# A one-layer hybrid encoder step: the raw weight loads of the projections go from SyncE's queue to POOL's

## The chip, the core and the metric

The kernel runs on one core of a Trainium2 chip. The metric is the time of one execution on the device in microseconds (us). Before the change three runs took 3268.99, 3278.84 and 3281.25 us; their median is 3278.84 us.

## The reference, cut to what matters

One step of a one-layer model on a prompt of 2048 tokens and a sample of 32 tokens, width 1024. Every matrix product with a weight is computed in float32 quality.

```python
z = rmsnorm(x, norm_mix_g) @ w_in                      # 1024 x 2560
q, k, v, zr = split(z, (512, 640, 768))
a_out = window_attention(q, k, v, ...)                 # 8 heads, windows of 64-token chunks
r_out, shift, S = rwkv7_mixer(zr, ...)                 # 8 heads, a recurrence over all tokens
x = x + concat(a_out, r_out) @ w_out                   # 1024 x 1024
x = x + memory_cross_attention(rmsnorm(x), mk, mv)     # w_cq 1024 x 512, w_co 512 x 1024
x = x + square(relu(rmsnorm(x) @ w_up)) @ w_down       # 1024 x 4096, 4096 x 1024
y = rmsnorm(x, norm_final_g)
```

The memory's keys and values are `rmsnorm(mem) @ w_mk` and `rmsnorm(mem) @ w_mv`. The recurrence `rwkv7_mixer` is serial over the tokens.

## The kernel before, in words

The 2080 tokens are kept transposed, width on the partitions. All projections but the MLP's work on four token groups of 512 or 544 tokens (`GROUPS`), each cut into two blocks of 256 or 272 columns. `dense` (line 299) runs one projection: for every weight unit it calls `load_w` (line 252) and then, for both blocks, `mm3` (line 230). A unit is 128 x 1024 numbers. Float32 quality comes from splitting a number into two parts of a shorter type: `mm3` does three matmuls per slice (high x high, high x low, low x high; lines 234 to 236), so a unit of 8 slices and 2 blocks is 48 matmuls into the tile `ps_z`.

`load_w` brings the weights in. For each half of a unit (512 columns) it takes a buffer `w_raw`, of which there are two (`RB` = 2), loads 128 x 512 float32 numbers from HBM by a DMA (line 257), and calls `split` (line 172): ACT copies the tile into the high part `w_h` (line 66), and POOL subtracts it from the raw tile and writes the low part `w_l` (line 69). When POOL is done, the raw buffer is free and its next load may start. The first two units of the kernel's first projection have their subtraction on DVE instead (`fast`). In the MLP `load_w` is called directly, with two raw buffers of its own (`fu`).

`zphase` (line 321) is the projection w_in; `ophase`, `cqphase` and `cophase` are w_out, w_cq and w_co; `memphase` does w_mk and w_mv. `PLAN` (line 35) lists in which sequence these are written down between the recurrence steps (R, `rwkv_tile`, 17 tiles of up to 128 tokens), the attention tiles (A) and the cross-attention jobs (X). Results go to HBM scratch (`zrw`, `zqkv`, `mscr`, `x2scr`, `qscr`, `cscr`, `x3scr`) and are loaded again by the next stage. An RWKV tile has a serial row of small transfers: it loads `zl`, `zin` and `zv`, stores `ab` to `lscr`, loads `lt` from it, stores `xt` to `xscr` and loads `td` from it (lines 533 to 678). On POOL it computes products for the tiles `z` and `bk` (lines 602 to 610) and the state `sn` (line 757), from `tp`, which DVE makes.

All DMAs are issued by SyncE (SP, `Q`). Each engine takes its instructions strictly in order, and so does each issuing queue: an instruction that waits holds all behind it on its engine. In which order the instructions of an engine stand is not the order of the code: a scheduler sets it before the run, by priorities (`setp`) and by its own estimate of when each operand is there. A change of the issuing engine therefore moves rows on all engines. The MLP follows the rest: six blocks of 352 or 320 tokens, `mup` and `mdn`.

Of the kernel before, what the change touches and what calls it, by code (L numbers as in the profile page):

```python
# [38 lines left out]
PSOL, PSER, RB, SNB = "s", "s", 2, 3  # L39
XB, WB, XS = 5, 2, 4  # L40
# [10 lines left out]
def hymba_step_kernel(  # L51
# [9 lines left out]
    V, G, S, T, Q = nc.vector, nc.gpsimd, nc.scalar, nc.tensor, nc.sync  # L61
# [19 lines left out]
    def pmm(name="pmm"):  # L81
        return psmm.tile([P, 512], F32, tag="pmm", name=name, bufs=PSB["pmm"])
# [89 lines left out]
    def split(xt, h, l, eng=None):  # L172
        act(h, xt)
        tt(l, xt, h.bitcast(F32), SUB, eng)
# [55 lines left out]
    def mm3(ps, wh, wl, xh, xl, nk):  # L230
        old = setp("m")
        for k in range(nk):
            a, b, c, d = wh(k), wl(k), xh(k), xl(k)
            T.matmul(ps, lhsT=a, rhs=c, start=(k == 0), stop=False)  # L234
            T.matmul(ps, lhsT=a, rhs=d, start=False, stop=False)  # L235
            T.matmul(ps, lhsT=b, rhs=c, start=False, stop=(k == nk - 1))  # L236
        setp(old)
# [10 lines left out]
    zp = stage1.enter_context(tc.tile_pool(name="zp", bufs=1))  # L248
    rctx = ExitStack()
    rp = rctx.enter_context(tc.tile_pool(name="rp", bufs=1))  # L250

    def load_w(pool, src, n=1024, bufs=3, tag="w", eng=None, rb=RB, raw=None):
        wh = pool.tile([P, n], F32R, tag=tag + "h", name="w_h", bufs=bufs)
        wl = pool.tile([P, n], F32R, tag=tag + "l", name="w_l", bufs=bufs)
        for i in range(0, n, 512):
            w = (raw or pool).tile([P, 512], F32, tag="wraw", name="w_raw", bufs=rb)
            Q.dma_start(w, src[:, i:i + 512])
            split(w, wh[:, i:i + 512], wl[:, i:i + 512], ENG[E7] if eng is G and i else eng)
        return wh, wl

# [38 lines left out]
    def dense(wsrc, units, xs, blks, evac, nk=KC, per=1, rs=None, fast=False):  # L299
        cols = nk * P  # L300
        if rs is None:
            rs = [None] * len(blks)
        for u in units:
            wh, wl = load_w(zp, wsrc[u], bufs=WB, eng=V if fast and u < units[0] + 2 else G)
            for j in range(per):
                ft = u * per + j
                for bi, (b0, nb) in enumerate(blks):
                    if callable(xs[bi]):
                        xs[bi] = xs[bi]()
                    xh, xl, r = xs[bi]  # L310
                    ps = pmm("ps_z")
                    mm3(ps[:, 0:nb], lambda k: wh[:, j * cols + k * P:j * cols + (k + 1) * P],
                        lambda k: wl[:, j * cols + k * P:j * cols + (k + 1) * P],
                        lambda k: xh[k // XS][:, k % XS, 0:nb], lambda k: xl[k // XS][:, k % XS, 0:nb], nk)
                    if rs[bi] is None and r is not None:
                        rs[bi] = r()
                    evac(ft, bi, b0, nb, ps, rs[bi])
# [3 lines left out]
    def zphase(g, units):  # L321
# [12 lines left out]
        def evac(ft, bi, b0, nb, ps, r):  # L334
# [26 lines left out]
            Q.dma_start(zqkv[g][:, ft, b0:b0 + nb] if ft < 6 else zrw[g][:, ft - 6, b0:b0 + nb], zo[:, 0:nb])  # L361

        dense(win, units, xs, blks, evac, rs=rs, fast=(g == 0 and 0 not in units))
        if 0 in units:
            zouts(g)
# [16 lines left out]
    def memphase():  # L382
        lab("mem")
        xs = [prep(memT.rearrange("(k p) t -> p k t", p=P), NMEM, "mem")]

        def evk(h, bi, b0, nb, ps, r):
            zo = zp.tile([P, NH], F32, tag="zo", name="zok", bufs=3)
            tt(zo[:, 0:nb], ps[:, 0:nb], r, MUL)
            Q.dma_start(kxs[:, h], zo[:, 0:nb])
            Q.dma_start(pmkT[:, h], zo[:, 0:nb])  # L390

        def evv(h, bi, b0, nb, ps, r):
            zo = zp.tile([P, NH], F32, tag="zo", name="zov", bufs=3)
            tt(zo[:, 0:nb], ps[:, 0:nb], r, MUL)
            pt = pmm("pvx")
            for m in range(2):
                T.transpose(pt[:, m * P:(m + 1) * P], zo[:, m * P:(m + 1) * P], ident)
            zv_ = zp.tile([P, NH], F32, tag="zo", name="zovt", bufs=3)
            act(zv_[:, 0:nb], pt[:, 0:nb])
            zv3 = zv_[:, 0:nb].rearrange("p (a b) -> p a b", a=2)  # L400
            Q.dma_start(vxs[:, :, h * P:(h + 1) * P], zv3)
            Q.dma_start(pmv[:, :, h * P:(h + 1) * P], zv3)

        dense(wmk, range(4), xs, [(0, NMEM)], evk)
        dense(wmv, range(4), xs, [(0, NMEM)], evv)
# [635 lines left out]
    for s_ in range(start[5] + 16):  # L1041
        up = []
        for i in range(2):
            u = (2 * s_ + i) % 3
            up.append(load_w(fw if u == 2 else fu, wup[2 * (s_ % 16) + i], bufs=1, tag=f"wu{u}", raw=fu))
        dn = [load_w(fw, wdn[2 * (s_ % 16) + i], bufs=3, tag="wd", raw=fu, eng=V)
              for i in range(2)]
        act_b = sorted((b for b in range(6) if start[b] <= s_ < start[b] + 16), key=lambda b: start[b])
        for b in act_b:
            if 0 < b < 3 and s_ == start[b]:  # L1050
                mprep(b)
            lab(f"M{b}.mm")
            us = mup(b, up)
            if s_ == start[b]:
                mres(b)
            if pend is not None:
                flush(pend)
            pend = (b, us, dn, s_ == start[b] + 15)
# [113 lines left out]
```

## Time and profile before

| what | value |
|---|---|
| median of 3 runs | 3278.84 us |
| the profiled execution | 3264.26 us, its span 3262.5 us |
| mean granted clock of TensorE (share of full speed) | 0.964 |
| PE busy | 3031.4 us (93%) |
| DVE busy | 1894.3 us (58%) |
| ACT busy | 1243.9 us (38%) |
| POOL busy | 1014.4 us (31%) |
| DMA, mean | 101 GB/s |

A profile tells for each engine when it worked and, where it stood idle, which other instruction ended the wait. PE is TensorE's matmul, DVE is VectorE, ACT ScalarE, POOL GpSimd, SP SyncE; SPq is SP's issuing queue. "A <- B: 10.0, 4, 3.1" in the view of waits means that A waited 10.0 us in all for B, 4 times, the longest 3.1 us. "out<-in" are the tiles that an instruction writes and reads. The chain of waits is followed back from the last instruction, at each step to what released it; its pieces add up to the span.

### The profile page before, as it was taken

What the parts mean: (1) busy time and instruction counts of PE and PEld (TensorE: products, weight loads), DVE (VectorE), ACT (ScalarE), POOL (GpSimd) and SP (SyncE); (2) the same over time, 40 slices, a digit from 0 to 9 for tenths busy, and PEclk for the clock granted to TensorE, in tenths of its full rate; (3) what the DMA queues carried; (4) which work ended last, traced back from release to release, by engine and by line L of the source; (5) the groups of instructions that cost most, each with busy time, mean ns of one, the idle gap of its engine ahead of it and who ended that gap; (6) DMA issues with size and microseconds to landing.
All of it is one profiled execution on the core that took longest, in us unless ns stands there. A gap on an engine that the chain in (4) does not pass through costs nothing.

```text
span 3262.5 us, 64715 instructions
## 1 busy us (share of the span) xinstructions
PE 3031.4 (93%) x25605; PEld 2837.5 (87%) x25605; DVE 1894.3 (58%) x4482; ACT 1243.9 (38%) x2824; POOL 1014.4 (31%) x1017
## 2 busy tenths in 40 slices
PE   8989888888988998998988999999999999999998
PEld 7877767777766987778877999999999999999998
DVE  4577788877776577764334544444445644444446
ACT  5355465444464454444453321222224322222223
POOL 3443354324254344425554411111113511011111
PEclk9999999999988999899989999999999999999999
DMA  5444353334443454346765211111113211111112
GB/s 170 133 114 109 104 147 110 104 87 123 120 137 101 131 158 127 111 124 195 247 217 171 67 50 42 46 46 52 39 46 115 66 43 52 40 52 52 46 46 91
DMA packets 336752, 328.95 MB, mean 101 GB/s; under 512 B 82320, under 2 KB 256064, under 8 KB 336448
## 3 DMA queue, kind: packets, MB, share of 16 engines
q1 hardware_dynamic: 336448, 324.81, 33.0%
q8 instruction: 201, 3.29, 0.4%
q14 instruction: 103, 0.84, 0.1%
HBM read 252.59 MB, written 72.39 MB: 100 GB/s over the span
## 4 chain that ended last, share of the span: by engine, by line
PE 62%; DVE 15%; DMA 11%; ACT 6%; issue 3%; POOL 2%; SPq 1%; DVEq 0%; POOLq 0%; ACTq 0%
PE ps_up L236 7%; PE ps_dn L1002 7%; PE ps_up L235 7%; PE ps_dn L1003 7%; PE ps_dn L1004 7%; PE ps_up L234 7%; PE ps_z L234 4%; PE ps_z L236 4%; PE ps_z L235 4%; DVE z L69 2%; DMA lt<-lscr 2%; DVE prd L69 1%; DMA lscr<-ab 1%; DMA xb<-x2scr 1%; ACT xh L66 1%
## 5 line engine op out<-in xcount | busy, mean ns | idle before, releaser
L234 PE MATMUL ps_z<-xh,w_h 128*128 128x256 f32 (+1 forms) x2368 | 716.7, 303 | 91.8 <-DVE zo L69 41.5
L235 PE MATMUL ps_z<-xl,w_h 128*128 128x256 f32 (+1 forms) x2368 | 705.9, 298 | 2.0 <-DVE xl L69 1.4
L236 PE MATMUL ps_z<-xh,w_l 128*128 128x256 f32 (+1 forms) x2368 | 704.0, 297 | 0.0
L66 ACT ACTIVATE w_h<-w_raw 128x512 fp32r<-128x512 f32 x576 | 344.7, 626 | 780.6 <-PE ps_up L235 258.5
L69 DVE TENSOR_TENSOR x<-ps_dn,x 128x352 f32<-128x352 f32 (+1 forms) x768 | 389.8, 516 | 367.4 <-PE ps_dn L1004 363.9
L69 POOL TENSOR_TENSOR w_l<-w_raw,w_h 128x512 fp32r<-128x512 f32 x300 | 393.1, 1325 | 608.8 <-ACT w_h L66 585.2
L234 PEld LDWEIGHTS ps_z<-xh,w_h 128*128 128x128 f32 x2368 | 470.4, 199 | 118.9 <-DVE zo L69 40.6
L69 POOL TENSOR_TENSOR rl<-rl 128x352 f32<-128x352 f32 (+1 forms) x192 | 162.1, 845 | 1137.3 <-ACT uh L66 1137.2
L1002 PE MATMUL ps_dn<-uh,w_h 128*128 128x352 f32 (+1 forms) x1536 | 492.9, 321 | 4.4 <-DVE x L69 3.3
L236 PE MATMUL ps_up<-fh,w_l 128*128 128x352 f32 (+1 forms) x1536 | 495.4, 323 | 1.2 <-DVE w_l L69 1.2
L1003 PE MATMUL ps_dn<-ul,w_h 128*128 128x352 f32 (+1 forms) x1536 | 491.0, 320 | 4.9 <-DVE ul L69 4.9
L234 PE MATMUL ps_up<-fh,w_h 128*128 128x352 f32 (+1 forms) x1536 | 493.2, 321 | 0.4 <-DVE zo L69 0.4
L235 PE MATMUL ps_up<-fl,w_h 128*128 128x352 f32 (+1 forms) x1536 | 491.1, 320 | 0.1
L1004 PE MATMUL ps_dn<-uh,w_l 128*128 128x352 f32 (+1 forms) x1536 | 490.7, 320 | 0.0
L235 PEld LDWEIGHTS ps_z<-xl,w_h 128*128 128x128 f32 x2368 | 470.4, 199 | 15.2 <-issue 7.4
L236 PEld LDWEIGHTS ps_z<-xh,w_l 128*128 128x128 f32 x2368 | 469.6, 198 | 15.5 <-issue 10.8
L69 DVE TENSOR_TENSOR w_l<-w_raw,w_h 128x512 fp32r<-128x512 f32 x276 | 198.0, 737 | 218.4 <-ACT w_h L66 217.9
L1003 PEld LDWEIGHTS ps_dn<-ul,w_h 128*128 128x128 f32 x1536 | 289.8, 189 | 5.5 <-DVE ul L69 5.2
L1002 PEld LDWEIGHTS ps_dn<-uh,w_h 128*128 128x128 f32 x1536 | 288.6, 188 | 6.8 <-DVE x L69 3.2
L236 PEld LDWEIGHTS ps_up<-fh,w_l 128*128 128x128 f32 x1536 | 288.4, 188 | 1.7 <-DVE w_l L69 1.5
L1004 PEld LDWEIGHTS ps_dn<-uh,w_l 128*128 128x128 f32 x1536 | 289.2, 188 | 0.2
L234 PEld LDWEIGHTS ps_up<-fh,w_h 128*128 128x128 f32 x1536 | 288.3, 188 | 1.2 <-DVE zo L69 0.6
(245 smaller groups left out, 4489.6 us busy)
## 6 DMA issues: line engine op xcount, KB each, us to landing
w_raw<-in_win SPq DMA_DIRECT2D x160, 256.0 KB, 2.9
w_raw<-in_wup SPq DMA_DIRECT2D x136, 256.0 KB, 2.7
w_raw<-in_wdn SPq DMA_DIRECT2D x136, 256.0 KB, 2.7
w_raw<-in_wout SPq DMA_DIRECT2D x64, 256.0 KB, 3.3
zrw<-zo SPq DMA_DIRECT2D x84, 128.0 KB, 1.9
lt<-lscr SPq DMA_DIRECT2D x34, 244.0 KB, 3.8
zin<-zrw SPq DMA_DIRECT2D x16, 512.0 KB, 3.9
w_raw<-in_wcq SPq DMA_DIRECT2D x32, 256.0 KB, 3.4
```

Of the source, the lines that this page charges most:

```text
L66: S.activation(out, in_, func, **kw)
L69: (eng or V).tensor_tensor(out, a, b, op=op)
L234: T.matmul(ps, lhsT=a, rhs=c, start=(k == 0), stop=False)
L235: T.matmul(ps, lhsT=a, rhs=d, start=False, stop=False)
L236: T.matmul(ps, lhsT=b, rhs=c, start=False, stop=(k == nk - 1))
L1002: T.matmul(ps[:, 0:n], lhsT=wh[:, ms], rhs=us[i][0], start=(i == 0), stop=False)
L1003: T.matmul(ps[:, 0:n], lhsT=wh[:, ms], rhs=us[i][1], start=False, stop=False)
L1004: T.matmul(ps[:, 0:n], lhsT=wl[:, ms], rhs=us[i][0], start=False, stop=(i == 1))
```

## The change

`load_w` gets a parameter `q`, the engine that issues the load of the raw tile. `dense` passes POOL (`G`) for it, and SP (`Q`) only for the first two units of the kernel's first projection. The calls in the MLP don't pass it and stay on SP.

```diff
-    def load_w(pool, src, n=1024, bufs=3, tag="w", eng=None, rb=RB, raw=None):
+    def load_w(pool, src, n=1024, bufs=3, tag="w", eng=None, rb=RB, raw=None, q=None):
         wh = pool.tile([P, n], F32R, tag=tag + "h", name="w_h", bufs=bufs)
         wl = pool.tile([P, n], F32R, tag=tag + "l", name="w_l", bufs=bufs)
         for i in range(0, n, 512):
             w = (raw or pool).tile([P, 512], F32, tag="wraw", name="w_raw", bufs=rb)
-            Q.dma_start(w, src[:, i:i + 512])
+            (q or Q).dma_start(w, src[:, i:i + 512])
             split(w, wh[:, i:i + 512], wl[:, i:i + 512], ENG[E7] if eng is G and i else eng)
...
         for u in units:
-            wh, wl = load_w(zp, wsrc[u], bufs=WB, eng=V if fast and u < units[0] + 2 else G)
+            wh, wl = load_w(zp, wsrc[u], bufs=WB, eng=V if fast and u < units[0] + 2 else G,
+                            q=Q if fast and u < units[0] + 2 else G)
```

SP's queue in the middle of the second group's w_in, before: the raw loads stand between the stores of results (`zo`) and the RWKV transfers.

```order
L655 DMA lscr_160_2407<-ab 64x8x64 x2
L660 DMA lt<-lscr_160_2407 64x976 x2
L257 DMA w_raw<-in_win 128x512
L361 DMA zrw_91<-zo 128x256
L257 DMA w_raw<-in_win 128x512
L797 DMA zq<-zqkv_86 128x4x128
L535 DMA zv<-zrw_90 128x4x32
L801 DMA kc__4098<-zqkv_86 128x128
```

The same RWKV tile on SP's queue after the change (lines after 304 have a number higher by one).

```order
L656 DMA lscr_160_2407<-ab 64x8x64 x2
L661 DMA lt<-lscr_160_2407 64x976 x2
L362 DMA zrw_91<-zo 128x256 x2
L536 DMA zv<-zrw_90 128x4x32
L534 DMA zl<-zrw_90 128x2x128
L362 DMA zrw_91<-zo 128x256
L675 DMA xscr_143<-xt 64x8x16 x2
```

No raw load is left between them, and the stores and loads stand closer together.

POOL in the same phase, before: subtractions of weights (`w_l`), the state `sn`, and RWKV's products.

```order
L69 TENSOR_TENSOR bk<-km,cs 64x8x64 x2
L69 TENSOR_TENSOR w_l<-w_raw,w_h 128x512 x2
L69 TENSOR_TENSOR sn<-tp,pcl 128x256
L69 TENSOR_TENSOR w_l<-w_raw,w_h 128x512 x2
L69 TENSOR_TENSOR sn<-tp,pcl 128x256
L69 TENSOR_TENSOR w_l<-w_raw,w_h 128x512 x4
L69 TENSOR_TENSOR z_4275<-zin,pp 64x4x64
L69 TENSOR_TENSOR z_4276<-zin,pp 64x4x64
L69 TENSOR_TENSOR bk<-kka,cs 64x8x64 x2
```

POOL at the same place after the change.

```order
L257 DMA w_raw<-in_win 128x512 x2
L69 TENSOR_TENSOR sn<-tp,pcl 128x256
L69 TENSOR_TENSOR w_l<-w_raw,w_h 128x512 x2
L257 DMA w_raw<-in_win 128x512 x2
L69 TENSOR_TENSOR w_l<-w_raw,w_h 128x512 x2
L257 DMA w_raw<-in_win 128x512
L69 TENSOR_TENSOR z_4275<-zin,pp 64x4x64
L69 TENSOR_TENSOR z_4276<-zin,pp 64x4x64
L257 DMA w_raw<-in_win 128x512
```

Issues of raw loads now stand on POOL behind the subtraction that frees their buffer, some of them directly in front of `sn` and `z` or behind them.

## Rows read from the trace of the kernel before

**Rows 1.** Busy time by stretch: us, then busy (instructions) by engine, clock, DMA
```profile
core 0: us, PE busy (x) PEld busy (x) DVE busy (x) ACT busy (x) POOL busy (x), PEclk, DMA share, GB/s
0.00:1790.00 1790.00, 1572.02 (x16419) 1384.61 (x16420) 1175.77 (x3155) 864.66 (x2060) 745.86 (x713) 0.94 0.47 138
1790.00:3262.00 1472.00, 1459.43 (x9188) 1452.86 (x9186) 718.48 (x1328) 379.26 (x765) 268.49 (x305) 1.00 0.17 55
```
**Rows 2.** Chain of waits, 0 to 1790 us: shares of the stretch by line
```profile
by line: PE ps_z L234 7.7%; PE ps_z L236 7.3%; PE ps_z L235 7.2%; issue 5.0%; DVE z L69 3.5%; DMA lt<-lscr 3.0%; DVE prd L69 2.2%; DMA lscr<-ab 2.1%; DMA xb<-x2scr 2.1%; ACT xh L66 2.0%; PE pA L225 1.8%; DVE xt L69 1.8%; DVE yb L72 1.5%; DM
```
**Rows 3.** DMA issues: queue, count, size of one, median us from issue to landing
```profile
w_raw<-in_win SPq DMA_DIRECT2D x160, 256.0 KB, 2.9
...
w_raw<-in_wout SPq DMA_DIRECT2D x64, 256.0 KB, 3.3
...
w_raw<-in_wco SPq DMA_DIRECT2D x32, 256.0 KB, 3.4
```
**Rows 4.** Tile w_raw, 0 to 1790 us: min/median/max ns, first to last start
```profile
L66 ACT ACTIVATE w_h<-w_raw x314: 611/624/659, 10.8 to 1789.9; 128x512 fp32r<-128x512 f32 x157
L69 POOL TENSOR_TENSOR w_l<-w_raw,w_h x300: 1257/1288/1809, 26.9 to 1760.8; 128x512 fp32r<-128x512 f32 x150
L257 SPq DMA_DIRECT2D w_raw<-in_win x160: 327/372/1699, 4.8 to 1161.6; - x160
```
**Rows 5.** Waits of SP's queue, 0 to 1790 us: total us, times, longest
```profile
SPq L257 <- POOL w_l L69: 228.0, 141, 7.8
...
SPq L655 <- ACT ab L66: 37.8, 12, 12.1
```
**Rows 6.** Waits of the engines, 0 to 1790 us
```profile
POOL sn L69 <- DVE tp L69: 111.5, 24, 15.3
...
ACT w_h L66 <- DMA w_raw<-in_win: 29.4, 23, 3.5
...
ACT w_h L66 <- DMA w_raw<-in_wout: 20.7, 12, 5.1
...
ACT w_h L66 <- DMA w_raw<-in_wco: 16.4, 11, 3.4
...
ACT w_h L66 <- DMA w_raw<-in_wmv: 9.0, 4, 4.5
...
ACT w_h L66 <- DMA w_raw<-in_wcq: 7.8, 5, 3.3
...
PE ps_z L234 <- ACT w_h L66: 11.9, 2, 11.4
```
**Rows 7.** Chain of waits, 104 to 136 us: start us, us, what
```profile
120.64 1.28 POOL w_l L69
121.94 0.33 SPq L257
...
122.38 2.52 DMA zl<-zrw
```
**Rows 8.** Chain of waits: the first and last moved load, and a blocked one
```profile
104.88 3.43 DMA w_raw<-in_win
...
1549.96 1.30 POOL w_l L69
...
1551.28 0.83 SPq L257
...
1552.16 0.42 SPq L463
...
1641.11 3.88 DMA w_raw<-in_wco
```
**Rows 9.** Groups of DVE instructions, 0 to 1790 us: count, busy us, mean ns
```profile
L853 DVE TENSOR_SCALAR sc<-sc,sm 128x256 f32<-128x256 f32 x120 | 59.5, 549 | 0.7
```
**Rows 10.** The page's costliest groups: busy us, mean ns, idle before
```profile
L234 PE MATMUL ps_z<-xh,w_h 128*128 128x256 f32 (+1 forms) x2368 | 716.7, 303 | 91.8 <-DVE zo L69 41.5
```

## The prediction

> **What bounds the kernel now.** I began with the busy times by stretch [rows 1]. They split the span at about 1790 us. In the second stretch, the MLP, PE is busy for 1459 of 1472 us, and its weight loads keep SP's queue: I take that stretch as unchanged. In the first, 1790 us with all projections, attention and RWKV, PE is busy for 1572 us, at a mean granted clock of 0.94, and idle for 218 us. No engine is full: DVE 1176 us, ACT 865, POOL 746 (42%). This is where the change acts.
>
> The chain of waits over the first stretch comes next [rows 2]. It is spread thin: the three dense matmul lines hold 22%, the rest is RWKV's arithmetic on DVE, PE's small matmuls, and transfers such as the load of the triangular factors (lt, 3.0%). No single wait rules the stretch, so only what lies on this thread counts.
>
> Then the loads of raw weights. A 256 KB load lands a median 2.9 to 3.4 us after its issue [rows 3]. SP spends a median 0.37 us on an issue; the ACT split after it takes 0.62 us, POOL's subtraction 1.29 us [rows 4]. Each half unit goes load, ACT, POOL, and its buffer (two exist) is then free for the next load. SP stands at line 257 until POOL's subtraction frees the buffer: 228.0 us in 141 waits, 1.62 us each, up to 7.8 us [rows 5]. That is the queue blocking which the change takes away. On the other side, ACT already finds a load not landed in 23 + 4 + 12 + 5 + 11 = 55 cases, 83.3 us, while PE itself shows only 11.9 us of waiting for w_h in two cases [rows 6].
>
> **The change, part by part.** It moves 300 issues (156 of w_in, 64 of w_out, 32 each of w_cq and w_co, 8 each of w_mk and w_mv) to POOL. Four first loads and all 272 MLP loads stay.
>
> *SP's queue is freed.* It loses 300 x 0.37 = 111 us of issuing and the 228.0 us of waiting. What of it is on the path? The chain shows two places where another load stands behind a raw load: POOL's subtraction of 1.28 us, then SP's issue of 0.33 us, then the zl load of an RWKV tile [rows 7], and once the same with 1.30 and 0.83 us in front of a cross-attention load [rows 8]. These are 1.6 and 2.1 us: a gain of 4 us. Nothing is the lower bound. The upper one is a mean wait of 1.62 us ahead of one transfer in each of the 17 RWKV tiles, 27 us. I stay with 4, because SP's own rows speak for it: where SP waits for the stores of lscr it has arrived early and waits for ACT (37.8 us) [rows 5], so these stores are not queued behind a raw load.
>
> *A load costs POOL something.* No row shows a DMA issue on POOL. The lower bound is SP's 0.37 us; the upper one is POOL's nearest row, the 1.29 us of the subtraction on the same tile [rows 4]. I take the upper, since it is the same engine and the same tile, and since the issue can't run beside the next subtraction. So each moved load lands 1.29 - 0.37 = 0.92 us later after its buffer falls free. On the chain of the first stretch 15 moved loads stand, the first at 104.88 us and the last at 1641.11 us [rows 8]: 15 x 0.92 = 14 us. The bounds are 0 and the 55 cases in which ACT is already waiting, 55 x 0.92 = 51 us. What hides the other 245 is that they land before ACT comes to them; the cover is gone where the slack was under a microsecond.
>
> The Trainium skill ("DMA: Bandwidth & Descriptors", section "Anatomy of one DMA — SWDGE (gpsimd) path") gives a fit for a DMA issued from this engine, 2.0 us plus the bytes over 436 GB/s, which for 262,144 bytes is an estimate of 2.6 us and so below the 2.9 to 3.4 us that the rows show on SP's queue; by it this term would be 0 rather than 14, and no run before the change can show which.
>
> *POOL gets fuller and is in order.* 300 x 1.29 = 387 us more make 1133 of 1790 us, 63%. The order shows issues put directly in front of RWKV's z products and of the sn step; the same holds for bk. A POOL row then meets an issue in front of it with a chance of 387/1790 = 0.22, and waits half of it, 0.65 us: 0.14 us. With 17 tiles and four such places each (two of z, two of bk), that is 10 us if all are on the path, 0 if none; I take 8, as the chain runs through the products for most tiles. The reverse also holds: a load is queued behind rows that wait. POOL waits for RWKV's tp in front of sn for 111.5 us, 24 times, 15.3 us at worst [rows 6]; the order has four issues directly behind an sn row. I leave this to the rivals.
>
> *The order moves.* The scheduler puts all engines' rows anew, PE's too. That has no price in a row; I allow a tenth of PE's 218 idle us, 22 us, to either side, in the range alone.
>
> The sum is -4 + 14 + 8 = +18 us. The profiled execution took 3264.26 us, 14.6 us under the median of the three runs, 3278.84 us; the change is added to the median: 3297 us.
>
> **Rivals.**
>
> *No change.* The issue on POOL costs little more than SP's, or the later landing is within the slack of the loads; then -4 + 0 + 8 = +4 us, 3283 us. For it: PE waits for a weight split in two cases only, and a dense unit of 48 matmuls of 0.30 us [rows 10] takes 14.5 us, against 2.9 to 3.4 + 0.62 + 1.29, at most 5.3 us, of load, split and subtraction. Against it: the 15 loads on the chain. The fit of the skill's DMA page, above, leads here.
>
> *Faster.* The blocking on SP is worth its upper bound: every RWKV tile gets one transfer 1.62 us earlier, -27 us, and POOL's issues fall into its 1044 us of idle time, 0 us: 3252 us. It decides if SP's wait at line 257 stands in front of one of a tile's serial transfers (zl, lscr, lt, xscr, td) in nearly all tiles. For it: 141 waits in 1790 us, one per 13 us. Against it: the chain shows it once for an RWKV tile.
>
> *Clearly slower: POOL as the blocked queue.* The wait that SP loses comes back on POOL, where it holds compute and loads together. If a third of the 111.5 us that POOL stands in front of sn is passed to loads and to the dense units behind them, 37 us, with the +18 that is +55 us, 3334 us. It decides when loads stand behind sn without a spare buffer; the order has four such places, at most 4 x 15.3 = 61 us.
>
> The Trainium skill ("SBUF — State Buffer", section "SBUF: two separate sides") states besides that a copy or tensor_scalar of DVE within SBUF locks POOL out of the port with which it writes a DMA's descriptors. As a mechanism of this kernel: the largest such DVE row takes 0.55 us, 120 times [rows 9]; 15 chain loads each delayed by a whole one would be 8 us, so 3305 us. I keep it within the slower case.
>
> **How the numbers follow.** Small loss of about 18 us: 0.45. No change: 0.28. Faster: 0.19. Clearly slower: 0.08. A measurement of this kernel can tell about 0.5%, 16 us, from no change, and the likeliest case lies close to that border; 0.08 of its 0.45 I count as ending within it. So faster is 0.19, same 0.28 + 0.08 = 0.36, slower 0.37 + 0.08 = 0.45. The range goes from the faster rival, 3252, to the slower one's 3334, with a few microseconds more at the top, 3338, for the port; the tenth of the idle time on either side of 3297 (3275 to 3319) is inside. The likeliest case's own range is 3283 to 3319.
>
> **What would show it.** In the profile after: the issues of raw loads appear on POOL with a duration (I say 1.29 us, bounds 0.37 and 1.29), and POOL's busy time or its waits grow by about 387 us in the first stretch. SP's wait at line 257 for POOL, 228.0 us, is gone there. ACT's wait for raw loads rises from 83.3 us to about 130. The second stretch stays at 1472 us within a few. The first grows from 1790 to about 1808 us with PE's busy time about the same. I am wrong if POOL's rows show no cost for an issue, if ACT's wait for loads falls, or if the RWKV chain's transfers start visibly earlier.

## The result and the profile after

The changed kernel takes 3293.91 us (median of 9 runs, 3286.76 to 3303.38) and the kernel before 3272.99 us (9 runs, 3267.73 to 3281.25). The ratio is 1.0059, with a 95% interval of 1.0048 to 1.0071: some 19 us slower. I had forecast 3297 us. One execution of pool_issue_three_buffers, a kernel further down, took 4883.40 us at a mean granted clock of 0.628 and is in no ratio.

Busy time by stretch, cut where the MLP's first matmul starts: the kernel before, then the one after (rows as in [rows 1]; the cut was 20 us later there).

```profile
core 0: us, PE busy (x) PEld busy (x) DVE busy (x) ACT busy (x) POOL busy (x), PEclk, DMA share, GB/s
0.00:1770.00 1770.00, 1558.23 (x16352) 1371.99 (x16352) 1156.00 (x3123) 860.44 (x2050) 735.69 (x707) 0.94 0.47 139
1770.00:3262.00 1492.00, 1473.21 (x9254) 1465.48 (x9253) 738.25 (x1360) 383.48 (x774) 278.66 (x311) 1.00 0.17 55
```
```profile
0.00:1797.00 1797.00, 1576.89 (x16352) 1388.87 (x16352) 1181.74 (x3122) 862.37 (x2050) 886.57 (x1007) 0.93 0.46 137
1797.00:3289.00 1492.00, 1473.21 (x9254) 1465.24 (x9253) 738.23 (x1360) 384.03 (x774) 278.20 (x311) 1.00 0.17 55
```

The second stretch is 1492 us in both, to a hundredth in PE's busy time. The whole loss, 27 us in this pair of profiled executions, lies in the first stretch, as forecast. The pair overstates it a little: the profiled execution before is 8.7 us under its kernel's median, the one after 2.4 us. In the first stretch PE executes the same 16352 matmuls, but is busy for 18.7 us more at a mean granted clock of 0.93 for 0.94 (a mixture of its 2.4 and 1.2 GHz levels; the lower one was granted for 256.0 us after and 221.9 us before), and idle for 8.3 us more (220.1 for 211.8). POOL's busy time grows by 150.9 us, DVE's by 25.7 us. That DVE's grows at all was in no step of mine.

The issues and landings of the moved loads come next, from the list of DMA issues (last column: median us from issue to landing) and the tile view of w_raw over the first stretch (min/median/max ns).

```profile
w_raw<-in_win POOLq DMA_DIRECT2D x156, 256.0 KB, 3.3
...
w_raw<-in_wout POOLq DMA_DIRECT2D x64, 256.0 KB, 3.4
...
w_raw<-in_wco POOLq DMA_DIRECT2D x32, 256.0 KB, 4.1
```
```profile
L69 POOL TENSOR_TENSOR w_l<-w_raw,w_h x300: 1255/1284/1742, 26.9 to 1788.4; 128x512 fp32r<-128x512 f32 x150
L257 POOL DMA_DIRECT2D w_raw<-in_win x156: 536/553/796, 19.6 to 1187.2; - x156
```

An issue holds POOL for 0.55 us, where I had said 1.29 [rows 4], and SP's took 0.37. The loads of these three weights land 0.1 to 0.7 us later than in [rows 3] (3.3 for 2.9, 3.4 for 3.3, 4.1 for 3.4 us); those of w_cq and w_mk land as before, at 3.4 and 3.0 us.

Then the waits, ACT's and SP's, over the first stretch (us in total, times, longest).

```profile
ACT w_h L66 <- DMA w_raw<-in_win: 67.5, 37, 9.6
...
ACT w_h L66 <- DMA w_raw<-in_wco: 30.0, 10, 5.9
...
ACT w_h L66 <- DMA w_raw<-in_wout: 17.1, 11, 4.4
...
ACT w_h L66 <- DMA w_raw<-in_wcq: 14.0, 6, 4.9
```
```profile
SPq L656 <- ACT ab L66: 75.2, 21, 14.6
```
```profile
PE ps_z L234 <- ACT w_h L66: 18.8, 4, 11.3
...
PE ps_z L236 <- POOL w_l L69: 5.0, 7, 1.4
```

With 1.5 us for w_mv, ACT stands 130.1 us for raw loads, in 65 cases, where it was 83.3 in 55 [rows 6]. SP's 228.0 us at line 257 [rows 5] are gone, and no gain shows: where SP stands for the data of lscr (line 656) it now does so for 75.2 us instead of 37.8 [rows 5] (49.3 in new_order_sp_issue below, which has the same order). I read this as SP arriving earlier and waiting for ACT. PE's own waits for the two halves of a weight come to 18.8 + 5.0 us; they were 11.9.

### The profile page after: what moved, and what is told of

It reads as the page before. It is cut to its first block, busy times and chain, and to the rows that moved or that the text cites. A ratio compares the mean times of both kernels' runs of the same rounds, so it can differ in the third digit from the quotient of the medians.

```text
span 3289.7 us, 64554 instructions
## 1 busy us (share of the span) xinstructions
PE 3050.1 (93%) x25605; PEld 2854.1 (87%) x25605; DVE 1920.0 (58%) x4482; ACT 1246.4 (38%) x2824; POOL 1164.8 (35%) x1317
## 4 chain that ended last, share of the span: by engine, by line
PE 59%; DVE 17%; DMA 12%; ACT 4%; issue 3%; POOL 3%; SPq 1%; DVEq 0%; ACTq 0%; POOLq 0%
PE ps_up L236 7%; PE ps_up L235 7%; PE ps_dn L1003 7%; PE ps_up L234 7%; PE ps_dn L1005 7%; PE ps_dn L1004 7%; PE ps_z L234 3%; PE ps_z L236 3%; PE ps_z L235 3%; DVE z L69 2%; DMA lt<-lscr 2%; DMA w_raw<-in_win 1%; DVE xt L69 1%; DMA lscr<-ab 1%; DVE prd L69 1%
## 5 line engine op out<-in xcount | busy, mean ns | idle before, releaser
L234 PE MATMUL ps_z<-xh,w_h 128*128 128x256 f32 (+1 forms) x2368 | 720.8, 305 | 116.0 <-DVE zo L69 43.3
L235 PEld LDWEIGHTS ps_z<-xl,w_h 128*128 128x128 f32 x2368 | 475.6, 201 | 19.7 <-issue 11.9
## 6 DMA issues: line engine op xcount, KB each, us to landing
w_raw<-in_win POOLq DMA_DIRECT2D x156, 256.0 KB, 3.3
w_raw<-in_wup SPq DMA_DIRECT2D x136, 256.0 KB, 2.8
w_raw<-in_wdn SPq DMA_DIRECT2D x136, 256.0 KB, 2.6
w_raw<-in_wout POOLq DMA_DIRECT2D x64, 256.0 KB, 3.4
w_raw<-in_wcq POOLq DMA_DIRECT2D x32, 256.0 KB, 3.4
```

## The experiments

The scheduler orders all engines anew when a load changes its queue, so the two kernels differ in more than the change says. To part the two, I fixed the order: a helper ties each instruction to the one ahead of it in a table of instruction numbers, engine by engine, with a dependency that orders but waits for no semaphore.

```diff
+def _pin(tc):
...
+    for engine, steps in json.loads(zlib.decompress(base64.b85decode(ORDER))).items():
...
+            if last is not None:
+                tc.add_manual_dep(i, last.name, dep, reason="pin")
+            last = i
```

"Old order" is that of the kernel before, "new order" that of the changed one. The helper stands ahead of the rest in the file, so that line numbers are higher in these kernels (line 257 is 273 to 279).

All twelve runs, with the ratio to the kernel before on the same chip. "First stretch" is the start of the first ps_up matmul; "ACT waits" is the sum of the rows "ACT w_h <- DMA w_raw" up to there, MLP loads left out; the busy times are the page's, of the whole span.

| kernel | us | ratio, 95% interval | first stretch | ACT waits, us (times) | DVE, POOL busy |
|---|---|---|---|---|---|
| before | 3272.99 | 1 | 1769.8 | 83.3 (55) | 1894.3, 1014.4 |
| after | 3293.91 | 1.0059, 1.0048 to 1.0071 | 1796.8 | 130.1 (65) | 1920.0, 1164.8 |
| old_order_pool_issue | 3312.7 | 1.0127, 1.011 to 1.0144 | 1820.5 | 157.9 (85) | 1915.2, 1167.3 |
| new_order_sp_issue | 3273.55 | 1.0007, 0.9996 to 1.0019 | 1773.9 | 59.0 (38) | 1900.1, 1007.2 |
| old_order_pool_early | 3322.54 | 1.0147, 1.0121 to 1.0173 | 1826.2 | 85.0 (54) | 1944.7, 1176.2 |
| old_order_sp_issue_pool_fill | 3287.74 | 1.0041, 1.0024 to 1.0058 | 1785.4 | 91.4 (57) | 1907.9, 1148.7 |
| new_order_pool_early | 3289.46 | 1.0051, 1.0033 to 1.007 | 1786.5 | 79.5 (47) | 1940.6, 1171.8 |
| old_order_sp_issue_tied | 3315.99 | 1.0133, 1.0112 to 1.0154 | 1817.3 | 174.3 (96) | 1895.6, 1009.2 |
| old_order_sp_issue_tied_fill | 3338.77 | 1.0206, 1.0183 to 1.0229 | 1842.1 | 183.5 (99) | 1904.4, 1145.3 |
| old_order_act_issue | 3288.99 | 1.0049, 1.0029 to 1.0069 | 1789.4 | 68.7 (43) | 1900.0, 1015.8 |
| pool_issue_three_buffers | 3287.9 | 1.0046, 1.0029 to 1.0062 | 1782.9 | 18.5 (20) | 1906.8, 1162.9 |
| sp_issue_three_buffers | 3250.35 | 0.9929, 0.9908 to 0.995 | 1747.3 | 11.7 (7) | 1878.4, 1004.6 |
| three_buffers_pool_order_sp_issue | 3271.71 | 0.9989, 0.9978 to 1.0 | 1765.2 | 6.0 (5) | 1895.4, 1010.5 |
| three_buffers_sp_order_pool_issue | 3281.13 | 1.0013, 1.0 to 1.0026 | 1782.8 | 43.3 (33) | 1886.8, 1160.0 |

### The issue or the order?

**old_order_pool_issue** is the change alone, in the order of the kernel before.

```diff
-            Q.dma_start(w, src[:, i:i + 512])
+            (q or Q).dma_start(w, src[:, i:i + 512])
...
+    _pin(tc)
```

> The order of every engine's rows is pinned to that of the kernel before; only the 300 raw loads are issued by POOL, each at the place in POOL's order at which the scheduler had put it in the whole program before. Theory A (the issue on POOL itself costs: later landings and a POOL row in front of others): 1.004 to 1.007 of the kernel before, +14 to +22 us, and ACT's wait for raw loads near the 129 us of the changed kernel. Theory B (the loss is the scheduler's new order): 0.998 to 1.002 of before. Theory C (SP freed is a gain that the new order hides): under 0.998.

Measured: 1.0127, 40 us slower, above every range that I had given: theory A's direction, at nearly twice its upper bound. **new_order_sp_issue** is the opposite: the changed kernel's order, with the loads on SP (the kernel before with only `_pin` and the table).

> The order of every engine's rows is pinned to that of the changed kernel; the 300 raw loads are issued by SP, each at the place at which the changed kernel's whole program has it. Theory A (the issue on POOL itself costs): 0.998 to 1.002 of the kernel before. Theory B (the new order costs): 1.004 to 1.008 of before. Theory C (the new order costs more than the change shows, and POOL's issue gives some of it back): over 1.008.

Measured: 1.0007, no difference from the kernel before that could be measured, and within theory A's range.

So the issue on POOL is the cause, and the new order by itself costs nothing. In the old order the issue costs 1.27%, in the new one 0.52% (1.0059 - 1.0007). The new order thus gives back 0.0127 - 0.0059 = 0.68%, some 22 us, of the 41 us that the issue costs. By what it gives them back was not shown; a first guess, below, gets no support.

### Which part of the issue?

**old_order_pool_early** moves each load on POOL to directly behind the subtraction that frees its buffer. In the old order 142 of 298 such loads stand behind the other half's subtraction too (two subtractions, then two loads), and in the new order 106; here none does. Only the table changes; POOL's rows where it does:

```diff
 w_l<-w_raw,w_h 128x512
+w_raw<-in_win 128x512
 w_l<-w_raw,w_h 128x512
-w_raw<-in_win 128x512
 w_raw<-in_win 128x512
```

**new_order_pool_early** is the same in the new order.

> The 300 loads are issued by POOL, all other rows of every engine stand in the order of the kernel before, as in old_order_pool_issue (3312.7 us, 40 over the kernel before); but each load stands on POOL directly behind the subtraction that frees its buffer, where there it mostly stood behind both subtractions of the weight (two subtractions, then two loads). Theory Q (queue place): the cost is that the first load of a pair waits on POOL behind the second subtraction (1.33 us and its wait for ACT), so the time falls by 20 us or more, to 3293 or below, with ACT's waits for raw loads near those of the kernel before (below 100 us in the first stretch; 150 with the old places). Theory O (occupancy): POOL's 0.55 us for each issue in front of the other half's subtraction and of other rows is what costs; the place hardly matters, 3305 to 3325 us. Theory L (the later landing alone, 0.3 us each): 3305 to 3315, ACT's waits as with the old places.

> The changed kernel with its own order on every engine, but each load on POOL directly behind the subtraction that frees its buffer. Theory Q: what the scheduler's order had not yet given back comes back, 3275 to 3285 us. Theories O and L: as the changed kernel, 3290 to 3297.

Measured: 1.0147 and 1.0051, in theory O's range (3305 to 3325) and half a microsecond under it (3290 to 3297). ACT's waits for loads fall as theory Q said, from 157.9 to 85.0 us and from 130.1 to 79.5, and the time does not follow: +0.2% in the old order and -0.08% in the new one, both less than the intervals are wide. So "the load comes too late, and that is all" falls, and the guess that the new order is better because fewer loads stand behind a second subtraction gets no support. By my reading, what the early load wins for ACT it takes from POOL, whose second subtraction now stands behind the issue, and from DVE: its busy time grows by another 29.5 us (1915.2 to 1944.7) and 20.6 us (1920.0 to 1940.6). Where that comes from, the last section shows.

The chains of waits of the first stretch fit this. These are new_order_sp_issue and then the changed kernel, which has the same order:

```profile
by line: PE ps_z L250 8.1%; PE ps_z L252 7.9%; PE ps_z L251 7.9%; issue 5.0%; DVE z L85 3.8%; DMA lt<-lscr 3.1%; DMA xb<-x2scr 2.6%; PE pA L241 2.2%; DVE prd L85 2.2%; DVE xt L85 1.9%; DMA lscr<-ab 1.6%; DVE sc L869 1.5%; ACT xh L82 1.5%; D
```
```profile
by line: PE ps_z L234 5.9%; PE ps_z L236 5.8%; PE ps_z L235 5.7%; issue 5.3%; DVE z L69 3.2%; DMA lt<-lscr 3.0%; DMA w_raw<-in_win 2.6%; DVE xt L69 2.5%; DMA lscr<-ab 2.4%; DVE prd L69 2.4%; PE pA L225 2.3%; DVE sc L854 2.3%; POOL w_l L69 2
```

Added up piece by piece, raw loads hold 36.2 us of the first chain (9 loads) and 80.7 us of the second (21), POOL's subtractions 19.1 and 38.8 us, and the issues themselves 5.6 us. In old_order_pool_early the loads are down to 47.5 us (12), but the subtractions stand at 41.5 us and the issues at 9.7. This is one chain of one execution each, so it tells where the loss lies and not what each part is worth.

**old_order_sp_issue_pool_fill** takes POOL's time without moving a load.

```diff
+    spare = const.tile([P, 470], F32, name="spare")
+    for _ in range(300):
+        G.memset(spare, 0.0)
+    _pin(tc)
```

> All loads on SP and every engine's order as in the kernel before; on POOL a memset of 128x470 numbers into an unused tile, some 0.55 us by the 128x256 one's 0.35, stands at each of the 300 places where old_order_pool_issue has a load. So POOL is held as long as by the issues, and no load moves. Theory O: 25 to 40 us slower than the kernel before (3298 to 3313). Theories Q and L: within 10 us of it (3270 to 3283).

```profile
L1083 POOL MEMSET spare<- x300: 480/492/919, 2.8 to 1770.4; 128x470 f32 x150
```

The fill takes 0.49 us each time, a little under an issue's 0.55, and makes the kernel 0.41% slower, 13 us. That lies under theory O's bounds (25 to 40) and just over the 10 that the others allowed: POOL's time is a part of the cost, about a third in the old order if a memset holds the other engines as an issue does, and not the whole.

**old_order_sp_issue_tied** takes no time on POOL, but ties each load on SP to the POOL row behind which old_order_pool_issue has it. **old_order_sp_issue_tied_fill** does both.

```diff
+            if i is not None and engine == "Pool" and str(i.engine).split(".")[-1] == "SP":
+                if last is not None:
+                    tc.add_manual_dep(i, last.name, tie, reason="tie")
+                continue
```

> All loads on SP, every engine's order as in the kernel before; each of the 300 loads also waits for the POOL row behind which old_order_pool_issue has it (for most the second subtraction of the weight, not the first). So the loads are tied to POOL's order, and POOL has nothing to issue. Theory T (the tie): a load that can't pass POOL's rows is what costs, 15 to 40 us slower than the kernel before (3288 to 3313). Theory P (what the issue itself does on POOL: its time, and DVE's instructions that wait through it): within 8 us of the kernel before (3265 to 3281).

> As old_order_sp_issue_pool_fill (a memset of 0.49 us on POOL at each of the 300 places, 3287.7 us), and each load on SP waits for its memset. That is the timing of old_order_pool_issue (3312.7 us) without an issue on POOL: the place in POOL's order, POOL's time, and DVE beside a POOL instruction are there; the landing over POOL's queue (3.4 us, not 3.1) is not. If place and time together are the cost: 3302 to 3315. If it lies in what only an issue on POOL has (its landing, its effect on DVE): 3283 to 3295.

Measured: 1.0133 for the tie, 1.0206 with the fill. The tie alone costs as much as the change in the same order, 43 us by the ratio (3315.99 us, 3 over theory T's range), so theory P falls, and ACT's wait for raw loads doubles. These are the two largest of its rows, then SP's wait for the subtractions.

```profile
ACT w_h L87 <- DMA w_raw<-in_win: 73.9, 53, 3.9
...
ACT w_h L87 <- DMA w_raw<-in_wco: 42.1, 18, 5.5
```
```profile
SPq L278 <- POOL w_l L90: 281.3, 98, 8.7
```

It is more than a share of the change, though. On SP a tied load also holds the transfers queued behind it: SP stands 281.3 us for POOL's subtractions, where it was 228.0 [rows 5], and 105.1 us more for other POOL rows, where it was 8.3; in the changed kernel SP is free. I take this to be why tie and fill together, 67 us by the ratio, overshoot both forecasts and the 41 of the issue that they imitate. I read 1.33% as an upper end for what the place in POOL's order costs; how much of the 1.27% it is stays open.

**old_order_act_issue** sends the loads through ACT instead, in the old order.

```diff
-                            q=Q if fast and u < units[0] + 2 else G)
+                            q=Q if fast and u < units[0] + 2 else S)
```

> The 300 loads are issued by ACT, at their place in the order of the kernel before; all else stands in that order. ACT has 1246 us of busy time, about as much as POOL with the issues, and DVE's waits show no ACT issue. If the cost is special to POOL (its 0.55 us issue, the 3.4 us landing, DVE held beside it): within 10 us of the kernel before, 3263 to 3283. If any engine that computes loses by it (the load waits for the rows ahead of it, and the rows behind wait for the load's buffer): 20 to 60 us slower, 3293 to 3333.

Measured: 1.0049, 16 us slower, between the two forecasts. The issue takes 0.33 us there:

```profile
L273 ACTq DMA_DIRECT2D w_raw<-in_win x156: 334/334/837, 19.0 to 1173.2; - x156
```

ACT waits less for raw loads than before (68.7 us for 83.3), and still the kernel is slower: both engines that compute paid for the move, POOL 2.6 times as much as ACT (1.27 to 0.49%).

### With the loads early

With a third raw buffer (`RB` 3 instead of 2, in line 39), a load is asked for half a weight earlier, and ACT hardly waits for it. `RB` is the default of `load_w`, so the MLP's raw buffers become three as well; its stretch is no shorter for that (1499.6 us in sp_issue_three_buffers, 1492.7 in the kernel before).

```diff
-PSOL, PSER, RB, SNB = "s", "s", 2, 3
+PSOL, PSER, RB, SNB = "s", "s", 3, 3
```

> The changed kernel with three raw buffers in the place of two, ordered anew by the scheduler. Theories Q and L: a load is asked for one half weight earlier, so lateness is covered: 3255 to 3280 us, ACT's waits for raw loads below 70 us in the first stretch (129 in the changed kernel). Theory O: POOL is held as before, 3285 to 3297.

> The kernel before with three raw buffers in the place of two, ordered anew by the scheduler. It stands beside pool_issue_three_buffers (3287.9 us), where a load is asked for one half weight earlier. Theory P: POOL's issues cost the same however early the loads are, so this one is 15 to 25 us faster than that one, 3263 to 3273. Theory T: with the third buffer the queue no longer matters, both at 3280 to 3290.

Measured: 1.0046 with POOL's issues, as theory O said (ACT's waits, 18.5 us, are below 70 all the same), and 0.9929 with SP's, 3250.35 us and so 13 us faster than any theory allowed. Their orders differ again, so I exchanged these too (`_pin` and a table, as above).

> Three raw buffers; every engine's rows stand in the order of pool_issue_three_buffers (3287.9 us), but the loads go over SP. In both three-buffer kernels ACT waits only some 20 us for raw loads in the first stretch, so a late load is not what parts them by 37 us. Theory P (issues on POOL hold POOL and DVE): 3247 to 3262 us. Theory S (the scheduler's order for POOL's issue is the worse one): 3275 to 3290.

> Three raw buffers; every engine's rows stand in the order of sp_issue_three_buffers (3250.4 us), but the 300 loads go over POOL, each at its place in that order. Theory P: 3275 to 3300 us, with ACT's waits for raw loads still below 50 us in the first stretch. Theory S: 3250 to 3265.

| ratio to the kernel before | loads on SP | loads on POOL | POOL's issue costs |
|---|---|---|---|
| two buffers, order made for SP (the kernel before's) | 1 | 1.0127 | 1.27% |
| two buffers, order made for POOL (the changed kernel's) | 1.0007 | 1.0059 | 0.52% |
| three buffers, order made for SP | 0.9929 | 1.0013 | 0.84% |
| three buffers, order made for POOL | 0.9989 | 1.0046 | 0.57% |

Neither theory holds alone: with POOL's order and SP's issue the time, 3271.71 us, lies between the two ranges, and with SP's order and POOL's issue, 3281.13 us, in theory P's. The issue costs 0.57 and 0.84%, though ACT waits no more than 43.3 us for loads in any of the four, and 18.5 or less in the pair with 0.57%. With three buffers the order made for POOL is itself the worse one, by 0.60% on SP and 0.33% on POOL: that it costs nothing holds for two buffers alone. In the order made for SP the third buffer lowers the issue's cost from 1.27 to 0.84%: so about a third goes with the late loads that the buffer covers, if the two orders may be compared, and two thirds stay. It does not cover them all: POOL's issue adds 31.6 us to ACT's waits there (11.7 to 43.3), and 74.6 with two buffers. How the two thirds divide between late loads that remain, POOL's time (0.41% for the fill) and DVE's longer rows was not separated.

The three-buffer kernel with the loads on SP, 3250.35 us, beats both: 0.71% under the kernel before (interval 0.5 to 0.92%). ACT's waits for raw loads there are 11.7 us in 7 cases, and the first stretch ends at 1747.3 us.

## Why the prediction was right in its sum and not in its terms

**The place of the loss: right.** The second stretch did not move, the first grew by 27 us (18 forecast); SP's wait for POOL vanished; ACT's wait for loads rose to 130.1 us (about 130 forecast). That last number was luck: it came from 55 waits of 0.92 us more, and both the price and the picture behind it are wrong, as the next two points say.

**The issue on POOL: mis-sized, 0.55 us for 1.29.** I took the upper bound from the subtraction's row. POOL's busy time grew by 150.9 us in the first stretch, not by 387. With 0.55 my own working gives (0.55 - 0.37) x 15 = 2.7 us for the later loads. POOL's 300 x 0.55 = 165 us are 9% of 1790, and 0.09 x 0.28 us x 68 places is 1.7 us. With -4 for SP the sum would be about 0 us, no change. So the method, fed with the right duration, would have missed: the hit was luck, a price that was too high for terms that were too few.

**"Each moved load lands 0.92 us later after its buffer falls free": the wrong picture.** On SP a load waits for the one subtraction that frees its buffer and for SP's own queue. On POOL it waits for every row ahead of it, and in the old order, for 142 of 298 loads, the next subtraction of 1.29 us is one of them. I had looked for such queueing at sn alone (the "clearly slower" rival); POOL's wait there fell, from 111.5 us [rows 6] to 88.6. The place that showed was the weight's own second half: loads tied to it on SP, with no issue on POOL, cost up to 1.33%. Placing the load ahead of that half won nothing, as then the half waits for the issue.

**"POOL gets fuller": 8 us, measured 13** with the fill in the old order. The size was about right, by a chance of meeting (0.22) that was too high and, as I read it, a number of places that was too low: I counted four rows of each RWKV tile and left out the subtractions themselves.

**SP's relief: 4 us, not shown.** SP waits longer for ACT at line 656, and its rows before had said that it arrives there early. How much SP's free queue is worth once loads are tied is open; tie and fill on SP cost 0.79% more than the issue on POOL, but the two kernels also differ in DVE's part (1904.4 and 1915.2 us busy) and in the landing.

**"The order moves": ±22 us with no sign.** It was the second largest term: +0.07% by itself, and 0.68% given back once the loads are on POOL. The scheduler put 36 loads fewer behind a second subtraction, but that alone is hardly the reason: old_order_pool_early has none there and is no faster. What gives the 0.68% back stays open. Without the new order the kernel would take 3313 us, 16 more than I said.

**PE's busy time "about the same": wrong.** Of the 27 us in the first stretch, 18.7 are the same matmuls at a lower mean clock. Idle PE time was not the whole price of a wait. Part of the 18.7 us is the difference between single executions; against new_order_sp_issue, in the same order, it is half and half: PE's busy time rises from 1566.4 to 1576.9 us, its idle time by 12.5.

**The rivals.** "No change" falls: the issue costs 0.52% even in the order made for it. "Faster" falls too: with SP free and all else in place the kernel is 41 us slower. The Trainium skill's port rule, which I kept within the slower case as loads delayed by DVE, shows the other way round, below. The Trainium skill's fit ("DMA: Bandwidth & Descriptors", section "Anatomy of one DMA — SWDGE (gpsimd) path"), an estimate of 2.6 us for this load, does not agree with the medians of 3.0 to 4.1 us from issue to landing measured here; the measurement decides.

## What to carry to other kernels

Before moving a DMA to an engine that computes, list what stands ahead of it on that engine and what behind: the load now waits for rows that it does not need, and they for its issue, and here placing it earlier only exchanged one for the other. When a scheduler orders the program anew, the comparison contains its answer to the change; fix the order once in each direction before giving the difference a cause. And where a queue is blocked by a buffer that is not yet free, try one more buffer first: here it gave 0.71%, and the move to another queue took 0.59%.

## What the chip showed that was not expected

A DVE instruction can be held through an issue on POOL and through the POOL instruction after it. The timeline of the changed kernel, then a like place of the kernel before (start, duration, engine, instruction):

```profile
1224.51 0.18 DVE L69 TENSOR_TENSOR xt<-xt,prd 128x24 f32<-128x24 f32 x1
...
1224.85 0.55 POOL L257 DMA_DIRECT2D w_raw<-in_wout  x1 [0.41 <-POOL w_l L69]
...
1224.96 1.81 DVE L69 TENSOR_TENSOR xt<-xt,prd 128x33 f32<-128x33 f32 x1
...
1225.42 1.29 POOL L69 TENSOR_TENSOR w_l<-w_raw,w_h 128x512 fp32r<-128x512 f32 x1
...
1226.81 0.19 DVE L69 TENSOR_TENSOR prd<-xt,lt 128x30 f32<-128x30 f32 x1
```
```profile
745.87 0.20 DVE L69 TENSOR_TENSOR xt<-xt,prd 128x36 f32<-128x36 f32 x1
...
746.09 2.52 POOL L69 TENSOR_TENSOR w_l<-w_raw,w_h 128x512 fp32r<-128x512 f32 x2 [0.77 <-ACT w_h L66]
746.11 1.31 DVE L69 TENSOR_TENSOR prd<-xt,lt 128x32 f32<-128x32 f32 x1
...
747.45 1.21 DVE L69 TENSOR_TENSOR xt<-xt,prd 128x32 f32<-128x32 f32 x1
```

The small tensor operation on xt takes 0.18 us at 1224.51. At 1224.96, 0.11 us after POOL began an issue, it takes 1.81 us and ends with the subtraction that follows the issue, 0.06 us behind it. Before, two like instructions begin beside two subtractions (2.52 us for both, so 1.26 us each). They take 1.31 and 1.21 us, and each ends within 0.1 us of the end of its subtraction. All 255 operations on xt in the first stretch, before and after (min/median/max ns):

```profile
L69 DVE TENSOR_TENSOR xt<-xt,prd x255: 143/185/1284, 181.1 to 1425.6; 128x30 f32<-128x30 f32 x25, 128x14 f32<-128x14 f32 x16, 128x24 f32<-128x24 f32 x16, 128x15 f32<-128x15 f32 x9
```
```profile
L69 DVE TENSOR_TENSOR xt<-xt,prd x255: 114/184/1810, 183.8 to 1454.3; 128x30 f32<-128x30 f32 x25, 128x14 f32<-128x14 f32 x16, 128x24 f32<-128x24 f32 x16, 128x15 f32<-128x15 f32 x9
```

The median stays (185 and 184 ns), the maximum goes from 1284 to 1810 ns.

It is not the issue by itself. I counted the tensor operations of DVE (tensor_tensor, tensor_scalar, scalar_tensor_tensor; groups of the same tiles and shape with ten rows or more) that begin during an issue in the first stretch, and of these the ones over 0.25 us longer than the median of their group. In the changed kernel it is 3 of 175 where another issue or a pause follows on POOL, and 12 of 41 where a computing row follows within 0.1 us; in old_order_pool_early 0 of 76 and 62 of 134. Of these 62, 22 would at their median have ended while the issue still ran. So it is the row behind the issue that holds DVE, and by the profile's times, which are rough on POOL, it does so from before it starts. With each load directly between two subtractions there are more such places; I take that to be a part of what the early orders lost.

The Trainium skill ("SBUF — State Buffer", section "SBUF: two separate sides") has GpSimd's instructions and some of DVE's, such as those with two inputs in SBUF, take a shared pair of ports for a whole instruction, with the other one blocked until it has ended. The rows beside a subtraction agree: 1.31 us in place of 0.20. That the hold begins during an issue ahead of the POOL instruction is what these rows add. The same section's warning, a DMA issued on this engine that can't write its descriptors while DVE holds the ports, shows little in the issues themselves: the longest of w_in is 0.80 us, 0.25 over the median. Whether a part of the later landings is such a wait was not tried.

Over all of DVE it is 20 us of busy time at a fixed order (1900.1 to 1920.0 in the new, 1894.3 to 1915.2 in the old), and 40 to 50 with the loads directly behind the subtraction (1900.1 to 1940.6, 1894.3 to 1944.7); the fill, a POOL instruction too, makes 14. What part of that is on the path was not tried by itself: every kernel with these holds also has POOL's issues. The chains of waits give a hint. DVE's rows on them that are over 0.25 us longer than their group's median lose 62.3 us by it in new_order_sp_issue and 65.1 after, 49.3 us in the kernel before and 62.9 in old_order_pool_early: some 3 us for the change at its own order, and 14 for the early loads.
